# A third half of the gates by seven block products, and the mixing steps in another order

## The chip, the core and the metric

The kernel runs on one core of one Trainium2 chip: TensorE (PE, with its weight loads PEld), VectorE (DVE), ScalarE (ACT), GpSimd (POOL) and SyncE (SP), which issues the loads of weights. The metric is the device time of one execution in microseconds (us). Each engine works through a queue of its own in a fixed order; an instruction that waits on a semaphore holds all that stand behind it on its engine.

## The reference, cut to what matters

One layer of an encoder trunk on x, 512 tokens by 1024 channels, all in float32: three token mixers (forgetting or "fox" attention, gated DeltaNet, stick-breaking attention, each with 4 heads of 128) are merged by three sigmoid gates, then a cross-attention into a memory and a gated feed-forward part follow. The gates are a dense product of the normalised input with a 1024 x 3072 matrix.

```
h = rmsnorm(x, norm_mix[l])
(fq, fk, fv, ff, gq, gk, gv, gb, ga, gz, sq, sk, sv, gates) = split_projection(h @ w_in[l])
...
yc = stick_breaking_attention(heads(sq, SB_HEADS), heads(sk, SB_HEADS), heads(sv, SB_HEADS))
g = jax.nn.sigmoid((gates + gate_bias[l]).astype(f32)).astype(x.dtype).reshape(B, S, N_BRANCH, D)
mixed = (g[..., 0, :] * (ya @ w_oa[l]) + g[..., 1, :] * (yb @ w_ob[l])
         + g[..., 2, :] * (yc @ w_oc[l]))
```

## The kernel before

Channels lie on partitions, tokens along the free axis (T = 512 columns). Every dense product takes its operands as a high and a low part (`hi`: an ACT copy to the reduced type fp32r; `lo`: a DVE subtraction, lines L187/L188 for a weight unit of 128 x 1024) and adds three products: hi by hi, hi by lo, lo by hi. A weight unit gives one output block of 128 channels; `project` (L227) with `mm3` (L213, L214, L216) makes 24 products of 512 columns of it.

**The gates.** A gate b (0 for fox, 1 for DeltaNet, 2 for stick-breaking) has eight output blocks, in two halves of four; steps A, B and C followed by 0 or 1 are the halves of gates 0, 1 and 2. Block m of gate b is `g24` for b = 2, m = 4 and so on. A plain half is four `project` calls and four multiplications by r_x (L486). Halves listed in `GATES_OF_SEVEN` go two blocks at a time through `gates_of_seven` (L822 to L865): weights and x are taken as 2 x 2 blocks, and seven half products (`half_product`, L254 to L270, each 12 products of 256 columns) take the place of eight. The sums of weight blocks that this needs are made on DVE:

```
w1, w2 = halves("1", a1)
s1, s3, s2, s4 = (awork(f"s{name}{i}") for i in (1, 3, 2, 4))
V.tensor_tensor(s1, a21, a22, ALU.subtract)
V.tensor_tensor(s3, a21, a11, ALU.subtract)
w5, w7 = halves("2", s1, s3)
```

Each is split anew (`whig` on ACT, L274; `wlog` on DVE, L275). The results are collected in three PSUM tiles pxg, pyg, pzg and combined on DVE (L857 to L862), then multiplied by r_x (L864). The sums of x that they use (xe, xf) come from `forms_of_x`, step T (L812 to L824), once. After each half its four sigmoids run in one go on ACT (`in_one_go`, L134 to L148: a table load, four sigmoids at L145, and the table load back at L139).

**The tiles `awork`.** A pool of eight buffers. The sums s1 to s4 (sg241 and so on in the program) take buffers of it, and so does each stick head, which fills all eight.

**A stick head** (`stick_head`, steps s0 to s3, L893 to L923) goes through four block rows j = 3 to 0, of 128, 256, 384 and 512 columns; for head 3 their PSUM tiles are sz33 to sz30. Each row: score on PE (L900); absolute value, exponential, logarithm on ACT (L902 to L904); DVE (L905); mask on POOL (L906); hi on ACT (L907); lo on DVE (L908); products with a triangle matrix on PE (L909, L910), and two more for each earlier row (L913, L914); exponential on ACT (L917) and mask on POOL. After row 0, PE makes `so` (L922).

**Other steps.** `mix` (a, b, c) multiplies a gate half by the branch's output product (`woa`, `wob`, `woc`; L879) and adds (L884); `delta_out` (y0 to y3) finishes a DeltaNet head. K, Q, V, k, q, v, R, p, e, l, n, z prepare and scan the DeltaNet heads, F and f are the fox heads, S projects for a stick head.

**The order.** The string `ORDER` gives the steps in program order. A scheduler then interleaves the instructions of all engines by that order and its own times for them, so that neighbouring steps mix; the queues below show the outcome.

Of the kernel before, what the change touches and what calls it, by code (L numbers as in the profile page):

```python
# [35 lines left out]
LOADS = (0, 1, 3, 2, 4, 5, 6, 7, 8, 9, 10)  # L36
KEYS_AFTER = (2, 3, 4, 5)
CROSS = "q0 q1 q2 q3 w0 w1 v w2 w3"
GATES_OF_SEVEN = ((1, 0), (1, 1))
ORDER = """K Q V R q F0 k v p0 f0 p1 S0 p2 p3 e F1 l0 l1 s0 l2 f1 F2 l3 f2 n0 F3 A0 C0 f3 n1 S1 S2 z n2 s1 s2 S3 a0 n3 T s3 A1 y0 a1 C1 c0 y1 B0 y2 c1 y3 B1 b0 b1"""  # L40
D = 1024
T = 512
KC = D // P
# [38 lines left out]
def build(nc, tc, ctx, x_t, mem_t, w, cols_d, const_d, unit_d, out_t, dbg=None):  # L82
# [139 lines left out]
    def project(u, xs, name, n=T):  # L222
        ps = dense_ps(name)
        mm3(ps[:, :n], split_unit(u), [block(k) for k in range(KC)], xs, True, True)
        return ps
# [259 lines left out]
    def normalized(dst, ps):  # L485
        V.tensor_tensor(dst, ps, r_x, ALU.mult)  # L486
# [379 lines left out]
    def gates(b, half):  # L866
        gate[b, half] = gs = [ptile(f"gate{b}{half}{i}") for i in range(4)]
        for i in range(4):
            m = 4 * half + i
            if (b, half) not in GATES_OF_SEVEN:  # L870
                normalized(gs[i], project(UNITS[f"gate{b}"] + m, xs, f"g{b}{m}"))
# [76 lines left out]

    for step in ORDER.split():
        step, h = step[0], int(step[1:] or 0)  # L950
# [530 lines left out]
```

## Time and profile before

| | |
|---|---|
| median of 3 runs | 1041.22 us (1040.79 to 1041.29) |
| profiled execution | 1040.94 us, its span 1039.2 us (1.7 us lie around the span) |
| PE busy in the span | 1025.6 us (99%) |
| DVE, ACT, POOL busy | 786.5 us (76%), 615.1 us (59%), 60.2 us (6%) |
| granted clock of PE, mean | 0.999 |

PE's idle time is 13.6 us in all. "Busy" counts an instruction from its start to its modelled end, and matmuls overlap, so a mean duration (about 0.4 us for 512 columns) is longer than the distance from one start to the next; where products follow one another, the distance is what each costs.

### The profile page before, as it was taken

The page shows a single profiled execution, that of the slowest core. Times are in us where ns is not written, and L with a number is a line of the kernel's source. Part 1 is how long each engine was busy: PE and PEld are TensorE (multiplying, and loading weights), DVE is VectorE, ACT ScalarE, POOL GpSimd, SP SyncE. Part 2 cuts the span into 40 slices and gives each one's busy share as a digit, 9 for nine tenths or more (in the row PEclk, how much of TensorE's full clock was granted, in tenths as well). Part 3 has the DMA queues.
Part 4 walks back from the last instruction along what each step waited for, and adds up shares of the span by engine and source line. Part 5 has one row for each costly group of instructions (what it writes and reads, how often), then busy time and mean ns, then how long its engine had stood idle before and what let it go on. Part 6 is the DMA issues. An engine that isn't in the chain of part 4 may idle for free.

```text
span 1039.2 us, 14990 instructions
## 1 busy us (share of the span) xinstructions
PE 1025.6 (99%) x5673; PEld 878.0 (84%) x5673; DVE 786.5 (76%) x1346; ACT 615.1 (59%) x1014; POOL 60.2 (6%) x116
## 2 busy tenths in 40 slices
PE   9999999999999999999999999999999999999998
PEld 7778888778887888789888888778889999989997
DVE  6696768788455447759988857679889988999873
ACT  6376757646343645647656757655678787855431
POOL 0000000101010000000000000000111111100000
PEclk9999999999999999999999999999999999999999
DMA  6323221211211112212254323142787878733441
GB/s 236 102 81 102 72 71 61 72 62 62 81 61 61 44 60 64 78 61 97 87 183 142 122 102 120 41 150 96 187 186 186 184 181 193 172 102 103 158 147 61
DMA packets 34344, 115.09 MB, mean 111 GB/s; under 512 B 3936, under 2 KB 4192, under 8 KB 33760
## 3 DMA queue, kind: packets, MB, share of 16 engines
q1 hardware_dynamic: 29088, 99.45, 28.5%
q0 software_dynamic: 4896, 14.42, 8.5%
q8 instruction: 44, 0.72, 0.3%
q10 hardware_dynamic: 288, 0.27, 0.1%
q14 instruction: 28, 0.23, 0.1%
HBM read 109.93 MB, written 4.19 MB: 110 GB/s over the span
## 4 chain that ended last, share of the span: by engine, by line
PE 95%; DVE 2%; ACT 1%; issue 1%; DMA 0%; SPq 0%; POOL 0%; DVEq 0%; POOLq 0%; ACTq 0%
PE dn L1280 8%; PE up L216 3%; PE up L214 3%; PE up L213 3%; PE g L213 3%; PE g L214 3%; PE g L216 2%; PE px L268 2%; PE px L270 2%; PE gk L470 2%; PE px L267 2%; PE dz L1280 2%; PE dx L1280 2%; PE f L213 1%; PE s L216 1%; PE s L214 1%
## 5 line engine op out<-in xcount | busy, mean ns | idle before, releaser
L187 ACT ACTIVATE whi<-wraw 128x1024 fp32r<-128x1024 f32 x109 | 115.3, 1057 | 125.2 <-issue 29.8
L188 DVE TENSOR_TENSOR wlo<-wraw,whi 128x1024 fp32r<-128x1024 f32 x109 | 133.0, 1220 | 43.6 <-ACT whi L187 23.9
L294 POOL DMA_DIRECT2D alo<-w x34 | 29.5, 866 | 417.9 <-ACT alo L293 407.4
L213 PE MATMUL g<-hh,whi 128*128 128x512 f32 x128 | 51.7, 404 | 1.6 <-DVE gate L486 1.6
L214 PE MATMUL g<-hl,whi 128*128 128x512 f32 x128 | 50.8, 397 | 0.0
L1280 PE MATMUL dn<-room,whi 128*128 128x256 f32 (+1 forms) x176 | 49.6, 333 | 0.0
L1177 DVE SCALAR_TENSOR_TENSOR uc<-u,cols,uc 128x511 f32<-128x511 f32 (+1 forms) x68 | 48.5, 749 | 1.0 <-ACT uc L1175 1.0
L293 ACT ACTIVATE alo<-wraw 128x1024 fp32r<-128x1024 f32 (+1 forms) x34 | 30.2, 888 | 16.3 <-DMA wraw<-w 15.1
L295 ACT ACTIVATE whi<-wraw 128x1024 fp32r<-128x1024 f32 (+1 forms) x34 | 30.3, 890 | 13.6 <-PE py L268 7.7
L275 DVE TENSOR_TENSOR sl<-s,sh 128x1024 fp32r<-128x1024 f32 x26 | 31.8, 1223 | 3.8 <-ACT sh L274 3.7
L216 PE MATMUL g<-hh,wlo 128*128 128x512 f32 x128 | 34.6, 404 | 0.0
L1280 PE MATMUL dn<-room,wlo 128*128 128x512 f32 (+1 forms) x128 | 34.0, 352 | 0.0
L1280 PEld LDWEIGHTS dn<-room,whi 128*128 128x128 f32 x176 | 29.8, 188 | 3.4
L213 PE MATMUL up<-xnh,whi 128*128 128x512 f32 x80 | 31.6, 395 | 0.0
L1280 PE MATMUL dn<-hidl,whi 128*128 128x512 f32 x80 | 31.6, 395 | 0.0
L214 PE MATMUL up<-xnl,whi 128*128 128x512 f32 x80 | 31.6, 394 | 0.0
L213 PEld LDWEIGHTS g<-hh,whi 128*128 128x128 f32 x128 | 24.1, 188 | 8.0 <-DVE gate L486 1.4
L274 ACT ACTIVATE sh<-s 128x1024 fp32r<-128x1024 f32 x26 | 27.3, 1051 | 4.8 <-PE px L268 1.9
L1175 ACT ACTIVATE uc<-u,cols 128x512 f32<-128x512 f32 x34 | 26.7, 809 | 4.5 <-DVE u L1250 3.6
L216 PEld LDWEIGHTS g<-hh,wlo 128*128 128x128 f32 x128 | 23.9, 188 | 6.2 <-issue 1.0
L214 PEld LDWEIGHTS g<-hl,whi 128*128 128x128 f32 x128 | 24.1, 188 | 5.1
L1280 PEld LDWEIGHTS dn<-room,wlo 128*128 128x128 f32 x128 | 23.8, 188 | 3.5
(1063 smaller groups left out, 3301.6 us busy)
## 6 DMA issues: line engine op xcount, KB each, us to landing
wraw<-w SPq DMA_DIRECT2D x166, 512.0 KB, 3.5
alo<-w POOLq DMA_DIRECT2D x21, 512.0 KB, 6.2
alo<-w POOLq DMA_DIRECT2D x13, 256.0 KB, 5.3
x<-x_t SPq DMA_DIRECT2D x8, 256.0 KB, 6.2
xr<-x_t SPq DMA_DIRECT2D x2, 1024.0 KB, 6.1
x_spill<-xr SPq DMA_DIRECT2D x2, 1024.0 KB, 4.3
x<-x_spill SPq DMA_DIRECT2D x8, 256.0 KB, 4.0
mem_sb<-mem_t SPq DMA_DIRECT2D x4, 256.0 KB, 3.9
```

The costliest lines, as they stand in the source:

```text
L187: S.activation(hi, raw, AF.Copy)
L188: V.tensor_tensor(lo, raw, hi.bitcast(F32), ALU.subtract)
L213: PE.matmul(ps, hi[:, b], xh, start=first and i == 0, stop=False)
L214: PE.matmul(ps, hi[:, b], xl, start=False, stop=False)
L216: mm = PE.matmul(ps, lo[:, b], xh, start=False, stop=last and i == len(xs) - 1)
L274: S.activation(hi, src, AF.Copy)
L275: V.tensor_tensor(lo, src, hi.bitcast(F32), ALU.subtract)
L293: S.activation(lo, src, AF.Copy, scale=-1.0)
L294: G.dma_start(lo, w[u, :, cols], accum_op=ALU.add)
L295: S.activation(hi, src, AF.Copy)
L1177: V.scalar_tensor_tensor(c[:, s:], u[:, :T - s], col("ffn_conv", 3 * j + 2 - s), c[:, s:], ALU.mult, ALU.add)
L1280: mm = PE.matmul(ps[:, z], lhs, rhs, start=first is None, stop=last, skip_group_check=True)
```

## The change

`GATES_OF_SEVEN` gets a third half, (2, 1), the second half of the stick-breaking branch's gate (step C1), and `ORDER` is written anew.

```
@@ -36,8 +36,8 @@
 LOADS = (0, 1, 3, 2, 4, 5, 6, 7, 8, 9, 10)
 KEYS_AFTER = (2, 3, 4, 5)
 CROSS = "q0 q1 q2 q3 w0 w1 v w2 w3"
-GATES_OF_SEVEN = ((1, 0), (1, 1))
-ORDER = """K Q V R q F0 k v p0 f0 p1 S0 p2 p3 e F1 l0 l1 s0 l2 f1 F2 l3 f2 n0 F3 A0 C0 f3 n1 S1 S2 z n2 s1 s2 S3 a0 n3 T s3 A1 y0 a1 C1 c0 y1 B0 y2 c1 y3 B1 b0 b1"""
+GATES_OF_SEVEN = ((2, 1), (1, 0), (1, 1))
+ORDER = """K Q V k R F0 f0 q v p0 p1 S0 F1 p2 p3 e s0 l0 l1 l2 f1 l3 F2 f2 F3 C0 A0 n0 f3 S1 n1 S2 s1 n2 z S3 s2 A1 n3 a0 s3 a1 y0 T C1 y1 y2 c0 B0 c1 y3 B1 b0 b1"""
 D = 1024
 T = 512
 KC = D // P
```

C1's four blocks lose 96 products of 512 columns and get 168 of 256 (PE's queue grows from 5392 to 5464 instructions); DVE's grows from 1348 to 1376, ACT's from 986 to 996. POOL's and SP's counts stay. PE's queue holds the same products in the same order from about 126 us to about 375 us of the trace, but for the two units A0 and C0 that change places; from the cross-attention on it is the same too.

**PE, at the last block rows of s3, before.** g24 and g25 are plain blocks of C1 (`whi53`, `wlo53` and so on are the two parts of their units), sz30 and sz32 block rows of stick head 3:

```order
L216 MATMUL g24_3932<-hh0_140,wlo53_3936 128x512
L900 MATMUL sz30_3672<-s03_3347,s13_3348 128x512
L216 MATMUL g24_3932<-hh0_140,wlo53_3936 128x512 x3
L216 MATMUL g24_3932<-hh1_223,wlo53_3936 128x512 x4
L213 MATMUL g25_3964<-hh0_140,whi54_3967 128x512
L214 MATMUL g25_3964<-hl0_141,whi54_3967 128x512
L213 MATMUL g25_3964<-hh0_140,whi54_3967 128x512
L214 MATMUL g25_3964<-hl0_141,whi54_3967 128x512
L213 MATMUL g25_3964<-hh0_140,whi54_3967 128x512
L909 MATMUL sz32_3640<-s301_3621,tri_r_329 128x256
L214 MATMUL g25_3964<-hl0_141,whi54_3967 128x512
L910 MATMUL sz32_3640<-s301_3621,tri_r_329 128x256
```

**PE, the same place, after.** pxg24 and pzg24 are PSUM tiles of C1's first pair, `whig241` and `wlog241` the parts of its first unit:

```order
L267 MATMUL pzg24_3966<-hh1_223,whig241_3936 128x256
L900 MATMUL sz30_3745<-s03_3266,s13_3267 128x512
L268 MATMUL pzg24_3966<-hl1_224,whig241_3936 128x256
L267 MATMUL pzg24_3966<-hh1_223,whig241_3936 128x256
L268 MATMUL pzg24_3966<-hl1_224,whig241_3936 128x256
L270 MATMUL pzg24_3966<-hh1_223,wlog241_3937 128x256 x4
L909 MATMUL sz32_3713<-s301_3694,tri_r_329 128x256
L910 MATMUL sz32_3713<-s301_3694,tri_r_329 128x256
L913 MATMUL sz32_3713<-s310_3695,tri_r_329 128x128
L914 MATMUL sz32_3713<-s300_3692,tri_r_329 128x128
L909 MATMUL sz31_3728<-s310_3695,tri_r_329 128x384
L910 MATMUL sz31_3728<-s300_3692,tri_r_329 128x384
```

and, at the end of that row of triangle products, the first product with a sum of weights (`whig242` is the high part of the sums sg241 and sg243):

```order
L914 MATMUL sz30_3745<-s301_3694,tri_r_329 128x256
L913 MATMUL sz30_3745<-s310_3695,tri_r_329 128x384
L914 MATMUL sz30_3745<-s300_3692,tri_r_329 128x384
L264 MATMUL pxg24_3964<-xeh0_3872,whig242_3946 128x256
L268 MATMUL pxg24_3964<-xel0_3873,whig242_3946 128x256
L267 MATMUL pxg24_3964<-xeh1_3888,whig242_3946 128x256
```

Before, 39 plain products of 512 columns stand between the score of sz30 (L900) and the second triangle product of sz31; after, seven of 256 columns stand between that score and the triangle products of sz32, all of sz31's and sz30's follow at once, and then C1's product with whig242.

**ACT, the same place, before and after** (s32x is the tile on which row x of head 3 is worked; sz32's exponential is L917 of s321):

```order
L903 ACTIVATE s320_3624<-s320_3624 128x384
L902 ACTIVATE s322_3625<-sz30_3672 128x512
L904 ACTIVATE s320_3624<-s320_3624 128x384
L903 ACTIVATE s322_3625<-s322_3625 128x512
L904 ACTIVATE s322_3625<-s322_3625 128x512
L907 ACTIVATE s310_3622<-s320_3624 128x384
L917 ACTIVATE s321_3626<-sz32_3640 128x256
L907 ACTIVATE s312_3623<-s322_3625 128x512
L187 ACTIVATE whi56_4031<-wraw56_4029 128x1024
L917 ACTIVATE s320_3624<-sz31_3655 128x384
L917 ACTIVATE s322_3625<-sz30_3672 128x512
```

```order
L903 ACTIVATE s320_3697<-s320_3697 128x384
L902 ACTIVATE s322_3698<-sz30_3745 128x512
L904 ACTIVATE s320_3697<-s320_3697 128x384
L903 ACTIVATE s322_3698<-s322_3698 128x512
L917 ACTIVATE s321_3699<-sz32_3713 128x256
L904 ACTIVATE s322_3698<-s322_3698 128x512
L907 ACTIVATE s310_3695<-s320_3697 128x384
L907 ACTIVATE s312_3696<-s322_3698 128x512
L917 ACTIVATE s320_3697<-sz31_3728 128x384
L274 ACTIVATE whig242_3946<-sg241_3940 128x512
L274 ACTIVATE whig243_3954<-wraw54_3934 128x512
```

L917 of s321, which reads sz32 after its triangle products, stood behind L904 of s322 and now stands ahead of it. The split of sg241 stands ahead of s322's last L917.

**DVE, the same place, after**, with the first sum of C1:

```order
L905 SCALAR_TENSOR_TENSOR s322_3698<-sz30_3745,s322_3698 128x512
L908 TENSOR_TENSOR s300_3692<-s320_3697,s310_3695 128x384
L908 TENSOR_TENSOR s302_3693<-s322_3698,s312_3696 128x512
L840 TENSOR_TENSOR sg241_3940<-wraw54_3934 128x512
L841 TENSOR_TENSOR sg243_3941<-wraw54_3934,wraw53_3932 128x512
L843 TENSOR_TENSOR sg242_3942<-wraw53_3932,sg241_3940 128x512
L275 TENSOR_TENSOR wlog242_3947<-sg241_3940,whig242_3946 128x512
```

The sum sg241 comes directly behind the last L908 of s3; in the program it waits for its buffer of the pool `awork`, which the triangle products of s3 read last. Before, the next sum of weights (sg101, of B0) stands four DVE instructions, two of them plain-gate splits of C1, further on.

**ACT, at B0's sigmoids, before and after** (whig142 to whig144 are parts of B1's first pair, gate100 to gate103 the half B0):

```order
L274 ACTIVATE whig142_4563<-sg141_4557 128x512
L274 ACTIVATE whig142_4563<-sg143_4558 128x512
L145 ACT_TABLE_LOAD
L145 ACTIVATE gate103_4163<-gate103_4163,cols_76 128x512
L145 ACTIVATE gate102_4162<-gate102_4162,cols_76 128x512
L145 ACTIVATE gate101_4161<-gate101_4161,cols_76 128x512
L145 ACTIVATE gate100_4160<-gate100_4160,cols_76 128x512
L139 ACT_TABLE_LOAD
L274 ACTIVATE whig143_4571<-wraw70_4551 128x512
L274 ACTIVATE whig144_4575<-sg142_4559 128x512
L274 ACTIVATE whig144_4575<-sg144_4560 128x512
```

```order
L274 ACTIVATE whig142_4693<-sg141_4687 128x512
L274 ACTIVATE whig142_4693<-sg143_4688 128x512
L195 ACTIVATE yb2h_4237<-yb2_4235 128x512
L274 ACTIVATE whig143_4701<-wraw70_4681 128x512
L145 ACT_TABLE_LOAD
L145 ACTIVATE gate103_4316<-gate103_4316,cols_76 128x512
L145 ACTIVATE gate102_4315<-gate102_4315,cols_76 128x512
L145 ACTIVATE gate101_4314<-gate101_4314,cols_76 128x512
L145 ACTIVATE gate100_4313<-gate100_4313,cols_76 128x512
L139 ACT_TABLE_LOAD
L341 ACTIVATE on3a_4661<-on3p_4654,cols_76 128x512
L274 ACTIVATE whig144_4705<-sg142_4689 128x512
```

whig143 stood behind the batch of sigmoids and stands ahead of it; whig144 is behind it in both, now after on3a.

## Rows read from the trace of the kernel before

**Rows 1.** The page, busy time of an engine (us, share of the span, instructions), and the first line of the chain that ended last, by engine.

```profile
PE 1025.6 (99%) x5673; PEld 878.0 (84%) x5673; DVE 786.5 (76%) x1346; ACT 615.1 (59%) x1014; POOL 60.2 (6%) x116
PE 95%; DVE 2%; ACT 1%; issue 1%; DMA 0%; SPq 0%; POOL 0%; DVEq 0%; POOLq 0%; ACTq 0%
```

**Rows 2.** The waits of PE, longest first: who waited, for what, us in total, times, the longest one.

```profile
PE g L213 <- DVE gate L486: 1.6, 2, 0.9
...
PE msc L1068 <- ACT mp L1072: 1.3, 1, 1.3
...
PE sz L900 <- ACT s L746: 0.2, 1, 0.2
```

**Rows 3.** Busy time by stretch of the span: the stretch, its length, then busy us (instructions) of PE, PEld, DVE, ACT and POOL, the granted clock, DMA share, GB/s. What PE lacks to the length is its idle time.

```profile
60.00:130.00 70.00, 69.90 (x318) 56.05 (x317) 52.87 (x81) 51.29 (x88) 1.96 (x8) 1.00 0.26 87
...
430.00:453.00 23.00, 23.00 (x106) 18.61 (x105) 13.42 (x20) 13.61 (x26) 1.95 (x6) 1.00 0.27 89
453.00:500.00 47.00, 47.00 (x284) 41.48 (x283) 38.14 (x62) 28.41 (x43) 0.29 (x1) 1.00 0.25 81
500.00:550.00 50.00, 48.95 (x292) 43.15 (x292) 46.41 (x78) 30.45 (x42) 0.00 (x0) 1.00 0.41 137
...
610.00:900.00 290.00, 287.46 (x1753) 256.09 (x1752) 240.97 (x394) 201.97 (x303) 28.66 (x34) 1.00 0.59 150
```

**Rows 4.** PE in order of time: start, us until the end of the group, line, output<-inputs, shapes, count. The first two are the third part of a plain gate-like product of 512 columns, one unit apart; the last two the first product of two half products of 256 columns, in B0.

```profile
55.83 2.02 PE L216 MATMUL gv<-hh,wlo 128*128 128x512 f32 x8
...
61.41 2.02 PE L216 MATMUL gv<-hh,wlo 128*128 128x512 f32 x8
...
475.81 0.29 PE L264 MATMUL pxg<-hh,whig 128*128 128x256 f32 x1
...
477.26 0.28 PE L264 MATMUL pzg<-hh,whig 128*128 128x256 f32 x1
```

**Rows 5.** DVE from 453 to 550 us, groups of one line, tile and shape: count, busy us, mean ns of one, idle before.

```profile
L188 DVE TENSOR_TENSOR wlo<-wraw,whi 128x1024 fp32r<-128x1024 f32 x9 | 11.0, 1221 | 0.5 <-ACT whi L187 0.5
L275 DVE TENSOR_TENSOR wlog<-sg,whig 128x512 fp32r<-128x512 f32 x16 | 10.5, 691 | 0.3 <-PE pxg L270 0.3
...
L840 DVE TENSOR_TENSOR sg<-wraw 128x512 f32<-128x512 f32 x4 | 2.8, 692 | 4.0 <-DMA wraw<-w 4.0
...
L857 DVE TENSOR_TENSOR gate<-pzg,vg 128x256 f32<-128x256 f32 x4 | 1.7, 424 | 1.8 <-PE pzg L270 1.8
```

**Rows 6.** All engines from 439 to 453 us in order of time, about the last block row of stick head 3 (s3): its score, the element-wise steps on it, and the triangle products. Start, us, engine, line.

```profile
439.85 1.02 PE L900 MATMUL sz<-s,s 128*128 128x512 f32 x2
440.30 2.19 PE L216 MATMUL g<-hh,wlo 128*128 128x512 f32 x7
...
441.33 0.59 ACT L902 ACTIVATE s<-sz 128x512 f32<-128x512 f32 x1
...
442.22 0.63 ACT L903 ACTIVATE s<-s 128x512 f32<-128x512 f32 x1
...
442.88 0.63 ACT L904 ACTIVATE s<-s 128x512 f32<-128x512 f32 x1
...
444.57 0.68 DVE L905 SCALAR_TENSOR_TENSOR s<-sz,s 128x512 f32<-128x512 f32 x1
...
445.38 0.49 POOL L906 TENSOR_SCALAR_AFFINE_SELECT s<-s 128x128 f32<-128x128 f32 x1 [0.27 <-DVE s L905]
...
445.90 0.63 ACT L907 ACTIVATE s<-s 128x512 fp32r<-128x512 f32 x1 [1.21 <-POOL s L906]
...
446.57 0.69 DVE L908 TENSOR_TENSOR s<-s,s 128x512 fp32r<-128x512 f32 x1 [0.85 <-ACT s L907]
...
450.37 0.33 PE L910 MATMUL sz<-s,tri_r 128*128 128x384 f32 x1
...
451.00 0.40 PE L909 MATMUL sz<-s,tri_r 128*128 128x512 f32 x1
...
452.10 0.34 PE L914 MATMUL sz<-s,tri_r 128*128 128x384 f32 x1
452.28 0.39 PE L213 MATMUL g<-hh,whi 128*128 128x512 f32 x1
```

**Rows 7.** DVE, ACT and PE from 506 to 516 us, where B0's sigmoids meet B1's weights. In brackets: idle time of the engine just before, and what ended it.

```profile
506.99 0.68 DVE L864 TENSOR_TENSOR gate<-gate,r_x 128x512 f32<-128x512 f32 x1
...
509.41 1.28 ACT L145 ACT_TABLE_LOAD   x1
510.70 2.56 ACT L145 ACTIVATE gate<-gate,cols 128x512 f32<-128x512 f32 x4
...
513.13 0.74 PE L270 MATMUL pxg<-xeh,wlog 128*128 128x256 f32 x4 [0.26 <-DVE wlog L275]
...
513.28 1.28 ACT L139 ACT_TABLE_LOAD   x1
514.58 0.63 ACT L274 ACTIVATE whig<-wraw 128x512 fp32r<-128x512 f32 x1
...
515.26 0.39 PE L264 MATMUL pyg<-xeh,whig 128*128 128x256 f32 x1 [0.79 <-ACT whig L274]
```

**Rows 8.** Busy time by stretch as in Rows 3, at the end of the span.

```profile
1034.00:1036.00 2.00, 1.34 (x6) 0.75 (x4) 0.62 (x1) 0.00 (x0) 0.00 (x0) 1.00 0.00 0
1036.00:1038.00 2.00, 0.00 (x0) 0.00 (x0) 0.07 (x1) 0.00 (x0) 0.00 (x0) 0.89 0.34 131
```

More of the change, by code (lines that the diff above doesn't have):

```diff
@@ L38 @@
 CROSS = "q0 q1 q2 q3 w0 w1 v w2 w3"
-GATES_OF_SEVEN = ((1, 0), (1, 1))
-ORDER = """K Q V R q F0 k v p0 f0 p1 S0 p2 p3 e F1 l0 l1 s0 l2 f1 F2 l3 f2 n0 F3 A0 C0 f3 n1 S1 S2 z n2 s1 s2 S3 a0 n3 T s3 A1 y0 a1 C1 c0 y1 B0 y2 c1 y3 B1 b0 b1"""
+GATES_OF_SEVEN = ((2, 1), (1, 0), (1, 1))
+ORDER = """K Q V k R F0 f0 q v p0 p1 S0 F1 p2 p3 e s0 l0 l1 l2 f1 l3 F2 f2 F3 C0 A0 n0 f3 S1 n1 S2 s1 n2 z S3 s2 A1 n3 a0 s3 a1 y0 T C1 y1 y2 c0 B0 c1 y3 B1 b0 b1"""
 D = 1024
```

## The prediction

> **What bounds the kernel now.** I read the page first: PE is busy for 1025.6 of 1039.2 us and 95% of the chain that ended last is PE's; DVE follows with 76% [rows 1]. So what counts is what PE's queue holds and when it stands still. The table by stretch shows where it stands still: in the stretch that the change rearranges, PE has no idle time from 430 to 500 us, where C1 stands today, 1.05 us from 500 to 550 and 0.1 us from 60 to 130, while DVE is busy for 13.42 of 23 us, 38.14 of 47 and 46.41 of 50 [rows 3]. The waits of PE name the longest: 1.6 us on the gates of L486, in a stretch whose order stays, and 1.3 us in the cross-attention, behind it [rows 2]. The 1.05 us are two gaps, 0.26 and 0.79, where B0's sigmoids hold ACT while B1's weights have to be split [rows 7]. So there is little idle time to win, and any new gap counts in full. The changed order is compared with the trace place by place, and each place is priced from rows.
>
> **The change part by part.** *Products.* 24 products of 512 columns take 61.41 - 55.83 = 5.58 us, a half product of 12 with 256 columns 477.26 - 475.81 = 1.45 us [rows 4]. Two plain blocks cost 11.16, seven half products 10.15; for C1's two pairs that is 22.3 against 20.3: **-2.0 us**, bounded by -2.0 and -2.2 if a product costs 0.120 or less.
>
> *Sums, splits and combinations.* A plain pair costs DVE two splits of 1.22 and two scalings of 0.69, 3.8 us; a seven pair four sums, five splits of 512 columns and two scalings of 0.69, one split of 1.22 and six steps of 0.42, 11.3 us [rows 5]. C1 gives DVE 15 us more. From 430 to 500 us DVE has 9.6 + 8.9 = 18.4 us idle [rows 3]: I cost it at nothing as a sum, the cover being PE's 70 us there. Where that fails is a rival below. ACT gets ten instructions more, at 0.63 us [rows 7] about 6 us, with 28 us idle in the same stretches [rows 3]. The steps moved ahead of 126 us have 0.1 us of PE's idle time to win [rows 3]; I take nothing, between a gain of 0.1 and a loss of 0.5, the size of the one wait of its kind that a head's score shows, doubled [rows 2].
>
> *C1 at the end of s3, first gap.* This is the term that decides. Today PE makes 39 plain products of C1, 39 x 0.2325 = 9.1 us [rows 4], between the score of sz30 and sz31's second triangle product. The last row of s3 thus has from 439.85 to 451.00 us for its steps [rows 6]. The steps need: score 1.02, ACT 0.59 + 0.63 + 0.63, DVE 0.68, POOL 0.49, ACT 0.63, DVE 0.69 [rows 6], 5.36 us, with some 0.06 for each of the seven handings-over (0.04 from L907 to L908, 0.13 from L905 to L906) 5.8 us. After the change PE has, from the same start, the score (0.45), seven products of 256 columns (0.84) and the triangle products of sz32 and sz31: five of sz31's six took 0.63 [rows 6], all together about 1.06. That is 2.35 us of work; then it stands before sz30's. The gap is 5.8 - 2.35 = 3.4 us at least. In the trace the same steps took from 439.85 to 447.26, 7.4 us, with plain splits between them [rows 6]; then it would be 5.1. L917 of s321 now stands ahead of L904 of s322 on ACT and waits for sz32's triangle products; all that is behind it waits as well. The plain splits are gone from there, so I take the lower end: **+3.4** (3.4 to 5.1).
>
> *Second gap.* sz30's products run to 452.44 [rows 6]. They release the tiles that sg241 needs; then come the sum (0.69, [rows 5]) and its split on ACT (0.63, [rows 7]), and only then the next product of PE's queue, pxg24 with whig242. Behind the triangle products PE has nothing ahead of it. Two handings-over make it 1.5 us from 452.44, while PE would have gone on at 452.28: **+1.6** (1.4 to 1.9). Today no sum is waited for here, and PE goes on with g26.
>
> *B0's first sum.* C1's four sigmoids now stand on ACT ahead of whig102, and the last scaling of C1 ahead of them. From C1's last product PE has 35 products of 512 columns and 24 of 256 until it needs whig102: 8.1 + 2.9 = 11.0 us. In that time DVE has two combinations (0.42), a split (1.22), a scaling, two sums, a product with woc00 and the last scaling (0.69 each) = 5.5 us, then ACT the batch from 509.41 to 514.58, 5.2 us [rows 7], and the split 0.63: 11.3. **+0.4** (0 to 1.2).
>
> *B1's weights.* The gaps of 0.26 and 0.79 go [rows 7]: **-1.05**, because whig143 now stands ahead of the batch. What is late next is whig144, behind the batch and a step on on3a of some 0.63: 0.79 + 0.63 less the half product that now covers it, 1.45, leaves nothing. But four more DVE instructions of 512 columns (0.69 each, about 2.5 us at their distance) stand ahead of gate103's scaling, which ended 507.67, 1.7 us before the batch began [rows 7]: 0.8 later. With the 0.6 of whig143 ahead of the batch in doubt: **+1.2** (0 to 1.8).
>
> *Sum.* -2.0 + 3.4 + 1.6 + 0.4 - 1.05 + 1.2 = +3.55 us. The profiled execution took 1040.9 us, so 1044.5; the median of the runs is 0.3 above it: **1044.8 us**.
>
> **The rivals.**
>
> *No new gap, PE's sum decides (faster).* The scheduler set the triangle products where its own times have them ready; if the chip's steps keep to those, the two gaps at C1 don't arise. For it: from 430 to 550 us PE today waits only 1.05 us [rows 3], so the laid-out places mostly hold. Against it: 2.35 us of cover for 5.8 us of steps. Without gaps at C1, B0 and B1: -2.0 - 1.05, **1038.2 us**. It decides for faster where all new waits together stay under 1.0 us (1039.1). The Trainium skill (Perfetto Trace Analysis, Identifying the Most-Contended Engine) says to optimise the engine of highest occupancy first, which here is PE; by it the products' saving would come through, with this rival's time.
>
> *The gap is paid back (no change).* While PE stands 5 us, DVE and ACT work ahead, and waits behind shrink: C1's and B0's lateness (1.6) and the 2.54 us of 610 to 900 [rows 3]. The sum would be -2.0 + 5.0 - 1.05 - 2.54 = -0.6: **1040.6 us**. Against it: the 1.3 us on L1072 [rows 2] belong to a chain of its own in the cross-attention, and the batches follow from C1's end, which is late itself.
>
> *The clock falls in the gap (slower).* PE's granted clock is 1.00 in every stretch that I read, the one with the wait of 1.3 us too [rows 2, 3]; when PE stops for good inside 1034 to 1036 us the next stretch shows 0.89 [rows 8], so it does fall without work. If it falls to the lower of its levels (1.2 GHz for 2.4) in a gap of 3.4 us, the sz30 products (1.3) and the first half product behind them (1.45) take twice their time: +2.4 us beyond the small terms, **1047.2**. The Trainium skill (TensorE: Matmul & The Clock Gate, What's actually happening) has the low level as the default and activity as what lifts it, which speaks for this; the trace agrees only at its end, and no row shows a gap of this length in the middle.
>
> *DVE becomes the bound (slower).* The 15 us fit into 18.4 us of idle time only if it lies in the right places. If 3 us don't fit, they come on top: **1047.8**. For it: from 500 to 550 DVE has 3.6 us left [rows 3]. Against: C1's gap gives it 5 us.
>
> **How the numbers follow.** Two executions differ by 0.5 us here, and 0.2% (2.1 us, so 1039.1 to 1043.3) is about what can be told from no change. The forecast case has 0.54; its own range, with all its terms at their ends, is 1042.9 (-2.2 + 3.4 + 1.4 - 1.05 = +1.6 on 1041.2) to 1048 (+6.9), of which 0.04 lies under 1043.3. The clock and DVE have 0.06 together, paying back 0.22, no gap 0.18. Faster: 0.18. Same: 0.22 + 0.04 = 0.26. Slower: 0.50 + 0.06 = 0.56. The range reaches down to the no-gap case, at 1038.4, and up to 1047.4; about 0.1 is left out on each side.
>
> **What the changed profile would show.** Right: PE idle for about 3.4 us before the triangle products of sz30 (or split between sz32, sz31 and sz30), with DVE's L908 as the releaser; then some 1.6 us before pxg24 with whig242, released by ACT L274; a short wait at B0's whig102; no wait before whig143, about 1 us before whig144; PE's busy time lower by 2 us; DVE's higher by 15; the granted clock 1.00. Wrong, if the triangle products follow their scores without a wait, because PE came late to C1's first products or because ACT and DVE had less to do there than the queues say; or if a wait of several us appears somewhere that I did not price, before A1 or in the rearranged stretch before 126 us above all.

## The result, and the profile after

The changed kernel takes 1044.26 us, median of 6 runs (1043.87 to 1046.31); the kernel before, beside it, 1041.17 us. The ratio is 1.0032, with an interval of 1.0022 to 1.0042: slower by 3.1 us. (Of most kernels here some executions are some 2 us longer than the rest, which is why ranges reach higher than intervals.) The profiled execution took 1043.95 us, its span is 1042.2 us, 3.0 us above the span before.

The page, busy time of each engine, as the first line of [rows 1]:

```profile
PE 1024.5 (98%) x5745; PEld 880.9 (85%) x5745; DVE 798.5 (77%) x1374; ACT 619.8 (59%) x1024; POOL 60.6 (6%) x116
```

PE's busy time fell by 1.1 us, and its idle time grew by 4.1, from 13.6 to 17.7: the change gained work and lost more waiting. Of the 4.1 us, 0.8 stand before the first dense product (a wait of 1.1 us for ACT's L462, 0.3 before) and cost nothing: PE's nine products ahead of it (L431) took 4.21 us before and take 3.64 now, and the next group starts at 7.16, for 7.29 before. The other 3.3 are taken up below. DVE's busy time grew by 12.0 us.

The waits of PE, as in [rows 2]:

```profile
PE g L213 <- DVE gate L486: 2.0, 3, 0.9
PE sz L909 <- ACT s L907: 1.6, 1, 1.6
...
PE pzg L264 <- ACT whig L274: 1.1, 1, 1.1
...
PE sz L910 <- DVE s L908: 0.6, 2, 0.3
```

Two waits on head 3's triangle products are new (1.6 once, 0.6 in two), and one on the gates of L486 (2.0 in three, from 1.6 in two). The wait for the split L274 is 1.1 us, for 0.8 before [rows 7]. The wait of the cross-attention is 1.3 us, as it was.

Busy time by stretch, as in [rows 3], with two short ones at the end (stretch, length, then PE, PEld, DVE, ACT, POOL, granted clock, DMA share, GB/s):

```profile
330.00:400.00 70.00, 68.36 (x367) 56.33 (x366) 30.65 (x62) 35.00 (x79) 4.51 (x12) 1.00 0.16 50
400.00:430.00 30.00, 29.56 (x142) 24.27 (x142) 26.77 (x47) 20.23 (x37) 2.49 (x5) 1.00 0.20 64
430.00:453.00 23.00, 20.85 (x110) 17.28 (x109) 13.38 (x22) 12.62 (x26) 2.55 (x7) 0.93 0.13 46
453.00:500.00 47.00, 47.00 (x344) 44.51 (x343) 45.42 (x79) 30.42 (x46) 0.00 (x0) 1.00 0.29 91
...
445.00:447.00 2.00, 2.00 (x9) 1.91 (x9) 1.84 (x4) 1.26 (x3) 0.00 (x0) 0.50 0.00 0
...
448.00:449.00 1.00, 1.00 (x8) 0.82 (x7) 1.00 (x3) 0.18 (x2) 0.24 (x1) 1.00 0.00 0
```

The first two stretches in the kernel before:

```profile
330.00:400.00 70.00, 69.11 (x367) 56.95 (x366) 33.49 (x67) 36.08 (x82) 3.78 (x14) 1.00 0.15 51
400.00:430.00 30.00, 29.76 (x150) 24.51 (x150) 23.22 (x41) 17.25 (x32) 3.26 (x4) 1.00 0.22 70
```

Of the 23 us from 430 to 453, PE worked in all before, and stands still for 2.15 now. The mean clock of that stretch is 0.93: from 445 to 447 us it is 0.50, the lower of the two levels (1.2 GHz), and from 448 us the higher one again (2.4 GHz). From 453 to 500 us DVE is busy for 45.42 of 47 us, and PE still does not wait there.

All engines at the last rows of s3, in order of time, as in [rows 6]:

```profile
438.34 1.02 PE L900 MATMUL sz<-s,s 128*128 128x512 f32 x2
438.80 0.68 PE L268 MATMUL pzg<-hl,whig 128*128 128x256 f32 x1
...
440.33 0.27 PE L914 MATMUL sz<-s,tri_r 128*128 128x128 f32 x1
442.18 0.44 PE L909 MATMUL sz<-s,tri_r 128*128 128x384 f32 x1 [1.58 <-ACT s L907]
442.96 0.45 PE L910 MATMUL sz<-s,tri_r 128*128 128x384 f32 x1 [0.34 <-DVE s L908]
...
444.51 0.79 PE L910 MATMUL sz<-s,tri_r 128*128 128x512 f32 x1 [0.23 <-DVE s L908]
444.55 0.82 DVE L840 TENSOR_TENSOR sg<-wraw 128x512 f32<-128x512 f32 x1
...
445.39 0.63 ACT L274 ACTIVATE whig<-sg 128x512 fp32r<-128x512 f32 x1 [1.00 <-DVE sg L840]
...
446.59 0.41 PE L264 MATMUL pxg<-xeh,whig 128*128 128x256 f32 x1
...
448.15 0.64 PE L270 MATMUL pxg<-xeh,wlog 128*128 128x256 f32 x4
```

Behind the score of sz30 (438.34) PE has the last of sz32's triangle products done at 440.60 (440.33 and 0.27) and then stands 1.58 us before sz31's, 0.34 and 0.23 us before the second products of sz31 and sz30. The releasers are ACT's and DVE's steps on those rows. The sum sg241 (L840, 444.55) starts right behind the last L908, while sz30's products run. These go at half the clock, and so do the products with whig242: eight in 1.56 us (446.59 to 448.15), 0.195 each, where 0.12 is usual [rows 4].

ACT and PE at B0's sigmoids, as in [rows 7]:

```profile
515.75 0.74 PE L270 MATMUL pxg<-xeh,wlog 128*128 128x256 f32 x4 [0.23 <-DVE wlog L275]
...
517.02 1.28 ACT L139 ACT_TABLE_LOAD   x1
...
519.58 0.39 PE L264 MATMUL pzg<-xfh,whig 128*128 128x256 f32 x1 [1.06 <-ACT whig L274]
```

whig143 is no longer waited for. whig144 is (1.06): it stands behind the batch, the table load of 1.28 us and on3a. PE's idle time here is 0.23 + 1.06 = 1.29 us, for 0.26 + 0.79 before [rows 7].

### The profile page after: what moved, and what is told of

Read it like the earlier page. It is cut to its first block, busy times and chain, and to the rows that moved or that the text cites. A ratio compares the mean times of both kernels' runs of the same rounds, so it can differ in the third digit from the quotient of the medians.

```text
span 1042.2 us, 15176 instructions
## 1 busy us (share of the span) xinstructions
PE 1024.5 (98%) x5745; PEld 880.9 (85%) x5745; DVE 798.5 (77%) x1374; ACT 619.8 (59%) x1024; POOL 60.6 (6%) x116
## 4 chain that ended last, share of the span: by engine, by line
PE 94%; DVE 2%; ACT 2%; issue 1%; DMA 0%; POOL 0%; SPq 0%; POOLq 0%; DVEq 0%; ACTq 0%
PE dn L1280 8%; PE up L216 3%; PE up L214 3%; PE up L213 3%; PE px L270 2%; PE px L268 2%; PE g L213 2%; PE gk L470 2%; PE g L214 2%; PE px L267 2%; PE g L216 2%; PE dz L1280 2%; PE dx L1280 2%; PE s L216 1%; PE s L213 1%; PE wo L214 1%
## 5 line engine op out<-in xcount | busy, mean ns | idle before, releaser
L187 ACT ACTIVATE whi<-wraw 128x1024 fp32r<-128x1024 f32 x105 | 111.2, 1059 | 129.9 <-issue 28.5
L188 DVE TENSOR_TENSOR wlo<-wraw,whi 128x1024 fp32r<-128x1024 f32 x105 | 128.1, 1220 | 45.4 <-ACT whi L187 19.6
L213 PE MATMUL g<-hh,whi 128*128 128x512 f32 x96 | 39.2, 408 | 2.6 <-DVE gate L486 2.0
L293 ACT ACTIVATE alo<-wraw 128x1024 fp32r<-128x1024 f32 (+1 forms) x34 | 30.2, 889 | 14.4 <-DMA wraw<-w 14.4
L214 PE MATMUL g<-hl,whi 128*128 128x512 f32 x96 | 37.9, 394 | 0.0
L274 ACT ACTIVATE sh<-s 128x1024 fp32r<-128x1024 f32 x26 | 27.3, 1051 | 4.7 <-PE px L268 1.8
L214 PE MATMUL up<-xfl,whi 128*128 128x512 f32 x64 | 25.4, 398 | 0.7 <-DVE xfl L206 0.7
L214 PE MATMUL s<-hl,whi 128*128 128x512 f32 x64 | 26.0, 406 | 0.0
L216 PE MATMUL g<-hh,wlo 128*128 128x512 f32 x96 | 25.7, 401 | 0.0
L213 PE MATMUL f<-hh,whi 128*128 128x512 f32 x64 | 25.7, 401 | 0.0
```

The source lines that it names most:

```text
L187: S.activation(hi, raw, AF.Copy)
L188: V.tensor_tensor(lo, raw, hi.bitcast(F32), ALU.subtract)
L213: PE.matmul(ps, hi[:, b], xh, start=first and i == 0, stop=False)
L214: PE.matmul(ps, hi[:, b], xl, start=False, stop=False)
L216: mm = PE.matmul(ps, lo[:, b], xh, start=False, stop=last and i == len(xs) - 1)
L274: S.activation(hi, src, AF.Copy)
```

## The experiments

A difference in time is taken against the kernel before on the same chip (median 1041.41, 1041.14 or 1041.16 us there). What the seven products cost in an order is taken from the ratios of two kernels.

**Which part of the change costs: C1's form or the order?** The first run has C1 in seven products in the order of before, the second the new order with a plain C1.

```
-ORDER = (the changed kernel's)
+ORDER = (before's)
```

> The three halves of the changed kernel with the ORDER of before. Theory (the seven form of C1 leaves s3's tail without cover, whatever the order): PE stands still at the triangle products of sz31 and sz30 for 2.5 to 3.5 us, the granted clock falls there, and the time is 1042.5 to 1044.5 us. Rival (the new order makes the loss, the products save 2 us): no gap over 1 us there, 1038 to 1040 us.

1043.74 us, ratio 1.0018 (1.0009 to 1.0026). The waits of PE at s3, then the microsecond from 444 us, with its granted clock:

```profile
441.69 0.44 PE L909 MATMUL sz<-s,tri_r 128*128 128x384 f32 x1 [1.57 <-ACT s L907]
442.47 0.69 PE L910 MATMUL sz<-s,tri_r 128*128 128x384 f32 x1 [0.34 <-DVE s L908]
```

```profile
444.00:445.00 1.00, 1.00 (x6) 0.89 (x4) 0.52 (x1) 0.49 (x1) 0.33 (x1) 0.50 0.00 0
```

With the old order the same gap stands before the same product with the same releaser, and the same fall of the clock behind it. Both come with C1's form, in either order. The clock does not fall in each execution, though: the mean granted clock is 0.998 in six of the eleven, as in the profiled one, and 1.000 in five. The six took 1043.56 to 1043.98 us, and three of the five 1043.47 to 1043.55 (the other two 1045.03 and 1045.20), so the fall itself seems to cost no more than some 0.3 us here.

```
-GATES_OF_SEVEN = ((2, 1), (1, 0), (1, 1))
+GATES_OF_SEVEN = ((1, 0), (1, 1))
```

> The ORDER of the changed kernel with C1 in plain products. Theory (C1's form makes the loss): no gap and clock 1.00 at s3's tail; the start about 0.8 us shorter and 330 to 430 us about 0.8 us longer, as in the changed kernel, so 1040.5 to 1042 us. Rival (the new order makes the loss): 1044 to 1046 us.

1043.02 us, ratio 1.0016 (1.0007 to 1.0025). The stretch of s3, and PE's waits elsewhere:

```profile
438.00:453.00 15.00, 15.00 (x68) 11.91 (x67) 8.02 (x12) 8.10 (x15) 1.24 (x4) 1.00 0.23 71
```

```profile
392.98 0.51 PE L213 MATMUL g<-hh,whi 128*128 128x512 f32 x1 [0.54 <-DVE s L486]
...
402.69 0.51 PE L213 MATMUL g<-hh,whi 128*128 128x512 f32 x1 [0.44 <-DVE gate L486]
...
484.00 0.50 PE L351 MATMUL on2p<-on2h,ones_r 128*128 128x512 f32 x1 [1.21 <-ACT on2h L195]
...
519.17 0.39 PE L264 MATMUL pyg<-xeh,whig 128*128 128x256 f32 x1 [1.40 <-ACT whig L274]
```

At s3 there is no gap and the clock stays at 1.00, as my theory had it. But the time lies outside the ranges of both theories and is not back at that of before: the order by itself costs 1.6 us. Its waits are 0.54 and 0.44 before plain products, 1.21 for ACT's split on2h of a DeltaNet output, which stands behind a step (L852) that itself waits for PE, and 1.40 before B1's products: 3.6 us for the 1.05 that they replace [rows 7]. Some 0.8 us of this comes back ahead of 170 us, as in the changed kernel (below); this trace does not show it, because its first products ran slowly (last section). By the ratios the seven products cost 1.9 us in the old order (1.0018) and 1.7 in the new one (1.0032 for 1.0016), with intervals of some 0.9 and 1.4 us to either side, so no difference between the two is shown. The waits are not the same ones, though: the 1.21 us at 484 are not in the changed kernel.

**Do the sums wait for their buffers?** My second gap said that sg241 waits for tiles of `awork` that s3 frees late. Here C1's four sums take tiles of another pool.

```
-        s1, s3, s2, s4 = (awork(f"s{name}{i}") for i in (1, 3, 2, 4))
+        own = (gwork,) * 4 if name[1] == "2" else (awork,) * 4
+        s1, s3, s2, s4 = (t(f"s{name}{i}") for t, i in zip(own, (1, 3, 2, 4)))
```

> The changed kernel, with the four sums of C1's pairs in buffers of the DeltaNet pool, not in those that s3 holds; PE's queue then has the twelve products with whig242 ahead of the triangle products of sz32, nothing else moves there. Theory (cover decides, and the clock falls because the gap is long): the gaps shrink from 2.8 us by 1.4, the clock stays at 1.00 or falls for less than 1 us, 1041 to 1042.5 us. Rival (the clock falls with any wait there): 1.4 us won alone, 1042.7 to 1043.2. If cover is not the cause: 1044.2 as the changed kernel.

1050.96 us, ratio 1.0079 (1.0063 to 1.0095): a miss of both theories. DVE and PE at s3 (line numbers are one higher from L841 on), and the clock:

```profile
441.82 0.69 DVE L841 TENSOR_TENSOR sg<-wraw 128x512 f32<-128x512 f32 x1 [0.91 <-DMA wraw<-w]
...
443.50 0.68 DVE L906 SCALAR_TENSOR_TENSOR s<-sz,s 128x512 f32<-128x512 f32 x1
443.64 0.44 PE L911 MATMUL sz<-s,tri_r 128*128 128x384 f32 x1 [0.88 <-DVE s L909]
```

```profile
450.00:452.00 2.00, 2.00 (x5) 0.86 (x4) 0.00 (x0) 0.00 (x0) 0.00 (x0) 0.50 0.00 0
```

With the buffer free, the scheduler put sums and splits earlier, as I meant: sg241 runs at 428.35, for 444.55 in the changed kernel, so the buffers do hold the sums back, through the order. But the next pair's sums moved too: its first sum and a split (441.82, 442.43) now stand ahead of L906 of the last row (443.50). The first waits 0.91 us for its weights' DMA and holds the row with it. From sz30's score to its second triangle product it takes 7.65 us (438.71 to 446.36), for 6.17 in the changed kernel, and the clock is low for longer (0.50 from 450 to 452). That is only a part of the loss: another 1.81 us stand before a product with a sum at 490.91, whose split waits behind a batch of sigmoids on ACT, and the clock falls a second time there (0.50 from 492 to 494 us). What stands in the queues ahead of the chain's steps costs more here than the buffers.

**What does the low clock cost?** 13 products of 256 columns behind sz32's triangle products and 8 of 128 ahead of sz31's L910 fill PE's gap. They write unused columns of the same tiles; some of head 3's sums are spoiled by that, and the output is not the reference's.

```
+            for i in range(8 if h == 3 and j == 1 else 0):
+                PE.matmul(whole[:, n:], tri_r[:, 0], eh[:, :P], start=True, stop=True, skip_group_check=True)
...
+            for i in range(13 if h == 3 and j == 2 else 0):
+                PE.matmul(whole[:, n:], tri_r[:, 0], e, start=True, stop=True, skip_group_check=True)
```

> The changed kernel with 13 products of 256 columns behind sz32's triangle products and 8 of 128 columns before sz31's L909 or L910, written into unused columns of the PSUM tiles and never read: about 2 us of work where PE stood still for 2.3. Theory (the low clock costs on its own): the clock stays at 1.00, the products from sz30's L910 to the first half product take 1.4 us less, a wait for whig242 of up to 0.5 us appears, 1042.8 to 1043.5 us. Rival (the low clock only fills the time in which PE would have waited for whig242): 1044.2 us as the changed kernel.

1043.69 us, ratio 1.0020 (1.0011 to 1.0028). PE at s3 (L919 and L912 are the fillers), and the clock:

```profile
440.32 1.75 PE L919 MATMUL sz<-s,tri_r 128*128 128x256 f32 x13
...
442.22 1.00 PE L912 MATMUL sz<-s,tri_r 128*128 128x128 f32 x8
...
444.59 0.50 PE L913 MATMUL sz<-s,tri_r 128*128 128x512 f32 x1 [0.23 <-DVE s L909]
...
446.12 0.39 PE L264 MATMUL pxg<-xeh,whig 128*128 128x256 f32 x1 [0.21 <-ACT whig L274]
```

```profile
446.00:448.00 2.00, 1.88 (x12) 1.54 (x12) 2.00 (x5) 1.60 (x4) 0.76 (x1) 1.00 0.00 0
```

The clock stays at 1.00 (0.999 or 1.000 in the mean of all eleven executions, for 0.997 or 0.998 in all six of the changed kernel), so it is PE's idle time there that lets it fall. The second product of sz30 still starts at 444.59 (444.51 in the changed kernel): the row's chain sets that moment, not PE. At full clock sz30's products are through early, and PE waits 0.21 us for whig242, the second gap in a small size. By the cross-attention (L1068) 0.4 us of it is left (654.59 for 654.98), and the medians lie 0.6 us apart, with intervals that overlap. The time lies between the two theories, 0.2 us above the first one's range. Of the 1.5 us by which the low clock stretches PE's products (below) most is not won back: at full clock PE reaches the products with C1's sums, and the step `so` behind them, ahead of what they wait for.

**Does plain work as cover help?** The plain half C0 is moved behind a1, next to C1, so that s3's last rows have plain products under them again; C1 once in seven products, once plain.

```
-... n0 F3 A0 C0 f3 n1 S1 S2 z n2 s1 s2 S3 a0 n3 T s3 A1 y0 a1 C1 c0 ...
+... n0 F3 A0 A1 f3 n1 S1 S2 z n2 s1 s2 S3 a0 n3 s3 a1 T C0 y0 C1 c0 ...
```

> The three halves of the changed kernel, with an ORDER in which A1 takes C0's early place and C0, in plain products, stands behind a1, so that C0's products lie under the steps of s3's last rows (8 us of PE work between the score of sz30 and its triangle products, where the changed kernel has 2.4). Theory (cover decides): no gap over 0.5 us at s3's triangle products, clock 1.00 there, the products' 2 us come through: 1038.5 to 1040.5 us. Rival (C1 in seven products starves PE by its sums wherever it stands): a wait for whig242 or wlog242 of 2 us or more remains and the time stays at 1042.5 to 1044.5.

1043.83 us, ratio 1.0021 (1.0012 to 1.0031). ACT and PE where C0's batch now stands and at B1, and the clock there:

```profile
442.17 0.63 ACT L274 ACTIVATE whig<-sg 128x512 fp32r<-128x512 f32 x1
...
442.85 0.38 PE L264 MATMUL pxg<-xeh,whig 128*128 128x256 f32 x1 [1.22 <-ACT whig L274]
...
518.11 0.38 PE L264 MATMUL pzg<-xfh,whig 128*128 128x256 f32 x1 [2.85 <-ACT whig L274]
```

```profile
516.00:518.00 2.00, 0.00 (x0) 0.00 (x0) 0.00 (x0) 1.99 (x4) 0.00 (x0) 1.00 0.33 135
```

No triangle product waits any more, and the clock is 1.00. But the first product with a sum waits 1.22 us: C0's batch holds ACT until 442.16, and whig242 stands behind it. Another 2.85 us stand at B1, behind B0's batch, and 1.15 at 482.89. The cover half of my theory is right, and the gain that it promised did not come. The rival is right on the time, and only half on the reason: the wait for whig242 is below its 2 us, and what PE lacks is the split on ACT, behind a batch of sigmoids, rather than the sums on DVE. The profile is of an execution with a mean clock of 0.999. In seven of the eleven it is 0.998 or 0.997, as in the changed kernel, so the clock seems to have fallen within them; no trace shows where.

> The same ORDER as plain_cover_seven with C1 in plain products. Theory: the difference to plain_cover_seven is what the seven products give when nothing waits on them, 1.5 to 2.2 us slower, so 1040.5 to 1042 us. Rival (the order alone makes the difference to before): no difference between the two, under 0.5 us.

1042.01 us, ratio 1.0004 (0.9995 to 1.0013): no different from before, and faster than plain_cover_seven, so both theories miss. PE's busy time on the two pages, the seven products first:

```profile
PE 1022.6 (98%) x5745; PEld 879.4 (84%) x5745; DVE 799.7 (77%) x1374; ACT 618.4 (59%) x1024; POOL 60.8 (6%) x116
```

```profile
PE 1024.7 (99%) x5673; PEld 877.1 (84%) x5673; DVE 787.1 (76%) x1346; ACT 614.3 (59%) x1014; POOL 60.8 (6%) x116
```

Both have the clock at 1.00 in the stretches of C1, so this pair gives the products' gain by itself: 1022.6 to 1024.7, **2.1 us**. The spans are 1040.8 and 1039.1: idle time 18.2 and 14.4, 3.8 us more. Of the 3.8, 3.5 are the waits above: 1.22, 1.15, and 1.10 of the 2.85 at B1, where 1.75 stand with a plain C1 too (at 515.92). In this order, too, the seven products cost 1.8 us net (ratios 1.0021 and 1.0004). With the plain C1 the mean clock is 0.998 in five of the eleven executions; the profiled one has 1.000.

**Can B1's waits be had back?** B0's sigmoids run with B1's, in one batch of eight behind B1, in three kernels: the changed one, plain_cover_seven and before.

```
-        in_one_go(gs, AF.Sigmoid, [col("gate_bias", 8 * b + 4 * half + i) for i in range(4)])
+        if (b, half) == (1, 0):
+            return
+        both = [(h, i) for h in ((0, 1) if b == 1 else (half,)) for i in range(4)]
+        in_one_go([gate[b, h][i] for h, i in both], AF.Sigmoid, [...])
```

> The changed kernel with B0's four sigmoids left until B1's, in one batch of eight. Theory (ACT, held for 5.2 us by B0's batch, is what keeps whig144 late): the wait of 1.06 us before the product with whig144 and the 0.23 before wlog142 go, the gap at s3 stays as it is, 1042.7 to 1043.4 us. Rival (DVE's sums are late there by themselves): the wait stays at 0.8 us or more and the time at 1044.

> plain_cover_seven with B0's and B1's sigmoids in one batch. Theory: its wait of 2.85 us before whig144 goes, 1039.7 to 1041 us on the runs that showed 1042.5, and the waits of 1.2 us for whig242 and of 1.2 in the second pair of C1 stay. Rival (DVE is the bound of that stretch): the wait moves to a later product and no more than 0.7 us is won.

> The kernel before with B0's and B1's sigmoids in one batch of eight: its two waits of 0.26 and 0.79 us at B1 go, 1039.9 to 1040.6 us against 1041.2. Rival (the longer batch at B1's end delays the last mixes): no gain, or up to 2 us slower, with a wait of PE behind b1.

1050.65 us (1.0092, 1.0078 to 1.0106), 1047.45 us (1.0064, 1.0050 to 1.0078) and 1047.91 us (1.0064, 1.0051 to 1.0076). All three miss the ranges of their theories, by more than 6 us, and no rival had reckoned with such a loss. In all three the wait before whig144 is gone (of B1's waits 0.35 or 0.25 before L270 stays, or none), so B0's batch on ACT is what holds it. ACT and PE behind B1 in the first:

```profile
541.16 5.01 ACT L145 ACTIVATE gate<-gate,cols 128x512 f32<-128x512 f32 x8 [1.19 <-DVE gate L864]
...
545.72 0.65 PE L213 MATMUL wob<-yb0h,whi 128*128 128x512 f32 x1 [4.42 <-DVE gate L882]
```

The batch of eight now ends at 546.2, and `wob`'s products of the mix wait for the gates behind it: 4.42 us here, 4.66 and 4.20 in the others (in the second, the waits of 1.2 us at 443 and 483 stay beside it). In or behind each of these waits the clock falls as well (0.50 from 546 to 548 us here). The early batch costs about 1 us at B1 and saves more than 4 here.

## Why the prediction was right, and where its terms were wrong

The time forecast was 1044.8, the median is 1044.26; slower was the likeliest sign. The mechanism, C1's short form takes the cover from s3's last rows and PE's order is held by their chain, is shown by seven_old_order (gap with the old order), new_order_plain_c1 (no gap with a plain C1), plain_cover_seven (no gap where plain products cover a short C1) and filled_gap (the chain's end stays when PE is kept busy). The terms:

*Products, -2.0.* 2.1 in the pair at full clock (plain_cover_seven and plain_cover_plain). Right. In the changed kernel PE's busy time shows 1.1, since products at the lower clock take longer.

*First gap, +3.4: 2.8 measured.* The chain from sz30's score to its L910 took 6.17 us (438.34 to 444.51), predicted 5.8. PE's work in it took 3.3 us, predicted 2.35; that was the mis-sized term. The seven products of 256 columns took 1.23 instead of 0.84: some 0.4 us pass behind the score, at 438.80. The triangle products, priced at 1.06, took 1.64: sz32's 0.41, sz31's six and sz30's first 1.23. Part of that stood in the rows of before already: sz32's four and sz31's six take 0.41 and 0.81 there, 1.22 in all, and sz30's first product, 0.23, was left out. With the score's 0.46 that is 3.33, and 6.17 - 3.33 = 2.8.

*Second gap, +1.6: not there.* The step that failed is "sz30's products release the tiles that sg241 needs". sg241 ran at 444.55, two microseconds ahead of their end (446.59), so its buffer was free by then, whoever read it last. Only the third sum (L843, 446.19) waits for sz30's products, by 0.16. The split of sg241 was done at 446.02, ahead of PE. What remains of this gap is the 0.21 us that filled_gap shows.

*In its place, the clock.* I gave its fall 0.06 together with DVE, and 1.00 as the sign of being right. It fell: behind idle times of 1.58, 0.34 and 0.23 us within four microseconds it stands at 0.50. The seven products from 444.51 took 2.08 us (in the fill run 1.15), and the eight behind them 1.56 instead of 0.96: 1.5 us. That this stood where I had put 1.6 us of waiting is a coincidence, and the sum was right partly by it. Gap and clock together are 4.3 us for 5.0 predicted; without the low clock 0.4 to 0.6 less (filled_gap), or some 0.3 by the executions of seven_old_order. The Trainium skill (TensorE: Matmul & The Clock Gate, What's actually happening) has activity as what lifts the clock; the fill run agrees, 1.00 where the changed kernel has 0.50.

*B0's first sum, +0.4: nothing.* PE has no idle time from 453 to 500 us. *B1, +0.15 net: +0.24.* whig143 ahead of the batch, and about 1 us before whig144 (1.06), as said; 1.29 us in all for 1.05.

*DVE at nothing.* Right: 45.42 of 47 us busy, and no wait of PE there. The work came out at 12 us for the 15 forecast, partly because instructions of 0.69 us start 0.60 apart (446.80, 447.40 and 448.00 in the changed kernel). The sums go where DVE has room, in the stretch that I named.

*What I did not price.* The same product (L594) starts at 164.59 us for 165.37 before, 0.8 us earlier; I had taken at most 0.1 for this stretch. From 330 to 430 us PE lacks 0.9 us more (68.36 and 29.56 for 69.11 and 29.76), in three places (new_order_plain_c1 has them too, at 364.40, 392.98 and 402.69):

```profile
362.21 0.49 PE L708 MATMUL sc<-st,gk 128*128 128x128 f32 x2 [0.46 <-DVE st L721]
...
390.80 0.50 PE L213 MATMUL g<-hh,whi 128*128 128x512 f32 x1 [0.54 <-DVE s L486]
...
400.51 0.50 PE L213 MATMUL g<-hh,whi 128*128 128x512 f32 x1 [0.44 <-DVE gate L486]
```

I had read that PE's order stays the same to 375 us and took nothing. In the traces it stays the same from 133 to 369 us, and DVE's to 374. The waits at 390.80 and 400.51 lie behind that, where the order of both engines changed and I had no term. The one at 362.21 lies ahead of it: the same instructions stand there in the same order, but a split on DVE (L188) ahead of L721 starts only 0.42 us earlier than before (360.67 for 361.09), where PE comes 0.78 us earlier. What holds it is open. The sum is -2.0 + 4.3 + 0.24 + 0.9 - 0.8 = +2.6; the span has +3.0. The 0.4 left over I have not placed. That the two unpriced terms nearly cancel is luck as well.

The rivals: *no new gap* is out, by the gap itself. The Trainium skill's rule to optimise the engine of highest occupancy first (Perfetto Trace Analysis, Identifying the Most-Contended Engine) does not hold here in that form: PE's work did fall, and the time rose in each of the three orders, by 1.7 to 1.9 us. *Paid back* is out: the 1.3 us of the cross-attention stayed, and the ledger of the same products stands at +3.0 there (L1068: 651.96 before, 654.98 after). *DVE the bound* is out, though sums_elsewhere shows how near it is when DVE's queue is filled in another order. *The clock* happened, at 1.5 us for the 2.4 of its price. (A small slip in the range: its lower end adds up to 1042.8, not 1042.9.)

Open: what exactly lets the clock fall. The traces show it behind three short waits within four microseconds and in or behind single ones of 4.20 to 4.66 us, and not behind single ones of 1.22 and 2.85 us in the one trace of plain_cover_seven; and seven_old_order has executions with the fall and without it. Nor have I traced why DVE, in the new order, comes late for 362.21, 390.80 and 400.51. No version tried beats the kernel before; plain_cover_plain equals it.

## What to carry to other kernels

Before a product is made cheaper, look at what runs under it: if a chain over the other engines ends behind those products, PE's queue has to hold as much work as that chain is long (here 6.2 us of steps, of which 3.3 were left under cover), and only what goes beyond is saved. A kernel whose main engine is at 99% is balanced by its order, so a rewrite of the order has to be priced in every stretch where any engine's queue changes, and not where PE's changes alone. Even a stretch whose queues stay the same gained a wait here (0.46 us at 362.21), for a reason that I have not found. A batch that holds an engine for 5 us moves a wait and does not remove it: each place tried for it here had its own victim.

## What the runs showed of the hardware

*The clock's fall does not go by the longest wait alone.* In the profiled execution of plain_cover_seven PE stands still for 2.85 us and has no product at all from 516 to 518 us, and the granted clock is 1.00 before, in and behind it; in the changed kernel 1.58 us with two short waits behind it gave 0.50. Nor is it the same each time: seven_old_order has a mean clock of 0.998 in six executions and 1.000 in five.

*Behind a score product about 0.4 us pass.* The 256-column product of 438.80, right behind L900, shows 0.68 us where 0.28 is usual [rows 4]; in before the seven of 512 columns behind the score took 2.19 us [rows 6], as against 2.02 for eight [rows 4], less one at 0.2325: 0.4 more.

*The first products run at nearly half speed for a time that differs from execution to execution.* In the profiled execution of new_order_plain_c1, PE's first dense products:

```profile
8.02 1.91 PE L470 MATMUL gk<-hh,glo 128*128 128x512 f32 x4
9.73 1.45 PE L470 MATMUL gk<-hl,ghi 128*128 128x512 f32 x4
11.02 1.09 PE L470 MATMUL gk<-hh,ghi 128*128 128x512 f32 x4
11.95 1.08 PE L470 MATMUL gk<-hh,glo 128*128 128x512 f32 x4
```

Four products in 1.71 us (8.02 to 9.73) are 0.43 each, four in 0.93 us (11.02 to 11.95) are 0.2325, as in [rows 4]. The spacing changes at 10.55 us, and the trace's first clock record, at 1.00, begins at 10.50; the 1.00 that a table of stretches prints ahead of it is no reading. In the other traces the change goes with that record too: 6.83 us and 6.72 in the kernel before, 7.40 and 7.30 in sums_elsewhere, 10.14 and 10.03 in after_one_batch; in the changed kernel the record begins at 4.21, and its first dense products (from 6.12) have the short spacing. So this looks like the lower level of the clock, although no record says so. The slow start sets this trace back by some 2 us: L594 starts at 166.78, and at 164.50 to 164.98 in the changed kernel, filled_gap and sums_elsewhere, which have the same order there. The DMA share does not explain it: it is 0.98 from 6 to 10 us here and 0.97 in the changed kernel.
